# Layer 1's third adaLN projection made on VectorE instead of TensorE, and another order of blocks in layer 1's output projection

## The chip, the cores and the metric

The kernel runs on 1 core of one Trainium2 chip. The metric is device microseconds of one execution, the median of several runs; less is better.

## The reference, cut to what matters

Two layers of a transformer-like block over 256 latent tokens (`x`) and 256 context tokens (`ctx`), 1024 channels wide. Each layer begins with a small product, the adaLN projection: one conditioning vector for the latent stream and one for the context stream, each times a 1024 x 6144 matrix. Its six pieces scale and shift what goes into the token mixer (`sh1, sc1`), gate what comes out (`g1`), and do the same for the MLP (`sh2, sc2, g2`). The last layer drops the context stream after its token mixer has read it.

```python
for l in range(2):
    with_ctx = l < 1
    mod_lat = silu(c) @ w_ada[l] + b_ada[l]            # 1 x 6144; the same for c_ctx
    sh1, sc1, g1, sh2, sc2, g2 = split(mod_lat, 6)
    h = x * (1 + sc1) + sh1
    z = h @ w_in[l]                                     # q, k, v of A and B; xr, yr of the LRU; gates
    ya, yb = windowed_attention(z), global_attention(z) # GQA, 8 heads each
    yc = bidirectional_rg_lru(conv(xr)) * gelu(yr)
    o = (ga * (ya @ w_br_a) + gb * (yb @ w_br_b) + gc * (yc @ w_br_c)) @ w_out[l]
    x = layernorm(ALPHA * x + g1 * o)
    h = x * (1 + sc2) + sh2
    x = layernorm(ALPHA * x + g2 * (square(relu(h @ w_ff1[l])) @ w_ff2[l]))
```

## The kernel before, in words

**Weights in blocks.** Every weight matrix is cut into blocks of 1 MB (`plan_units`, a list in the order of use). A block is loaded into one of 3 `raw` buffers (`emit_dma`, L181, on SP's queue), then split into a high and a low part, `whi` and `wlo` (`queue_split`, L197: the cast on ScalarE, in layer 1's LRU half of it on VectorE; the subtraction on VectorE, L128), and TensorE takes three products per pair of tiles (high·high, high·low, low·high). `take` (L225) hands out a block and calls `prefetch` (L240), which calls `ada_step`, loads the block after next and queues the split of the next one. While `ada_q` (below) holds anything, `prefetch` loads up to two blocks ahead, otherwise three.

**The planner's clock.** `mm` (L89) adds an estimate to `self.pe` for every matmul: 0.42 per column of the moving operand, at least 107. Everything that is spread over time by hand hangs on this clock, not on the chip's: `tick` (L248) is called once per three matmuls, and starts pieces of splits and background steps. A block of 48 matmuls with 512 columns makes 48 x 215 = 10,322 units; with 256 columns (one stream only, as in layer 1 behind the LRU's inputs) 5,161.

**The adaLN projections.** Each layer's 6144 columns go in three projections of 2048 columns (blocks 0 to 3, 4 to 7 and 8 to 11 of 512 columns). A projection has 8 steps, one per 128 rows of the matrix. A step loads 1 MB into a `raw` buffer (the same three as the weights; `raw_ada`, L276), and then either

- on VectorE (`dve` = 1): 8 adds of 128x512, `ada_acc = raw_ada * silu + ada_acc` (L293; in the first step a plain product, L291), and after the eighth step `sums`: 8 matmuls with `pick` that sum over the partitions; or
- on TensorE (`dve` = 0): 4 matmuls per step straight from `raw_ada` (`mms`).

`ADA` says which projection is queued where. Before: layer 0's second and third at the start of layer 0's merge (`bra0`), layer 1's first and second at the start of layer 0's MLP (`mlp0`), both on VectorE; layer 1's third (blocks 8 to 11: `sc2` and `g2`) at the first gates of layer 1 (`ga1`), in its attention, on TensorE. `ada_step` (L335) runs one step at a `prefetch`, if the planner's clock has come to `ada_at`: it issues the adds still left of the step before, loads the next one, and sets `ada_at` to now plus the pace of the layer whose matrix it is. `tick` issues the adds one by one, the first 3000 units after the load, then one per gap:

```python
self.ada_at, self.ada_next, self.ada_gap = self.pe + pace, self.pe + 3000, (pace - 3000) / 8
```

**The order of the stages.** Layer 0: LRU, attention together with the merge, output projection, MLP (32 blocks of 512 columns: 16 of `f1`, 16 of `f2`). Layer 1: `lru` (L733) takes `xr0 xr1 yr0 yr1 kvA xr2 yr2 kvB xr3 yr3 qA0 qA1` in this order, and between them runs the LRU's chain on ScalarE, VectorE and GpSimd (`finish`, L758); then the attention, paired with `qB0 qB1` and the merge; the output projection (`wout`); the MLP. `xr` and `kv` are for both streams (512 columns), the others of layer 1 for the latent one.

**Layer 1's output projection and its tail.** `unit` (L1192) multiplies one half `h` of the 1024 rows of `w_out` for one block of 128 tokens `tb`; the two halves add up in one PSUM bank, and after the second `residual` (L1181) multiplies by the gate, adds, and takes the statistics, on VectorE. `tail_units` (L1290) does so for the last 512 columns (`keys[0]` and `keys[1]` are the halves), then `ln_z` (L1220) normalises, `ln_t` transposes on TensorE, and `ln_h` makes the MLP's input. The order before was tokens 2 half 0, tokens 2 half 1, tokens 3 half 0, tokens 3 half 1.

Of the kernel before, what the change touches and what calls it, by code (L numbers as in the profile page):

```python
# [47 lines left out]
class Kern:  # L48
# [220 lines left out]
    def ada_queue(self, l, blocks, dve):  # L269
# [18 lines left out]
        def add(k, j, s):  # L288
            acc, w, c = st["acc"][s][j], st[k][:, j, :], self.silu[:, k, s:s + 1]
            if k == 0:  # L290
                self.nc.vector.tensor_scalar(acc, w, c, None, op0=ALU.mult)  # L291
            else:
                self.nc.vector.scalar_tensor_tensor(acc, w, c, acc, op0=ALU.mult, op1=ALU.add)  # L293
# [24 lines left out]
        for k in range(KD):  # L318
            if dve:
                self.ada_q.append((lambda k=k: dma(k),  # L320
                                   [lambda k=k, j=j, s=s: add(k, j, s) for j in range(4) for s in range(2)],
                                   sums if k == KD - 1 else None, self.ADA_PACE[l]))
            else:
                self.ada_q.append((lambda k=k: dma(k), [], lambda k=k: mms(k), 0.0))

    ADA_PACE = (9500, 18000)

    ADA = (('bra0',0,4,1),('bra0',0,8,1),('mlp0',1,0,1),('mlp0',1,4,1),('ga1',1,8,0))

    def ada_start(self, at):  # L330
        for a, l, b, dve in self.ADA:
            if a == at:
                self.ada_queue(l, range(b, b + 4), dve)
# [956 lines left out]
    def tail_units(self, l, which, keys, xs):  # L1290


        final = l and which == 2
        if final:
            self.lnr = self.ln_rows(l, which)
        else:
            self.hn = [(self.g("h_hi", F32R), self.g("h_lo", F32R)) for _ in range(KD)]
        if l:
            ws = []
            for tb, j in ((2, 0), (2, 1), (3, 0), (3, 1)):  # L1300
                if tb == 2:
                    ws.append(self.take(keys[j]))
                self.unit(keys[j], ws[j], xs, (tb,), True)
                if j and not final:
                    self.ln_z(tb)
                elif j:
                    self.output(tb)
            if not final:
                self.ln_t(2)
                self.ln_t(3)  # L1310
                self.ln_h(l, which, 1)
                self.ln_late = lambda: None
        else:
            ws = [self.take(keys[0]), self.take(keys[1], prefetch=False)]
            for tb in range(2):
                for key, w in zip(keys, ws):
                    self.unit(key, w, xs, (tb,), True)
                if tb:
                    self.ln_t(0)
                self.ln_z(tb)  # L1320
            self.unit(keys[0], ws[0], xs, (2,), True)
            self.ln_t(1)
            self.ln_h(l, which, 0)
            self.unit(keys[0], ws[0], xs, (3,), True)
            self.prefetch()
            for tb in (2, 3):
                self.unit(keys[1], ws[1], xs, (tb,), True)
                self.ln_z(tb)

            def late():  # L1330
                self.ln_t(2)
                self.ln_t(3)
                self.ln_h(l, which, 1)

            self.ln_late = late
        if not final:
            self.h = self.hn
# [262 lines left out]
```

## Time and profile before

| | us |
|---|---|
| median of 3 runs | 1507.12 (1506.59 to 1509.21) |
| the profiled execution | 1507.38 |
| its span | 1505.6 |
| PE busy | 1455.2 (97%) |
| DVE busy | 1154.4 (77%) |
| ACT busy | 772.2 (51%) |
| POOL busy | 292.7 (19%) |

The span is the time from the first to the last instruction of one execution that the profiler recorded. PE is TensorE, DVE VectorE, ACT ScalarE, POOL GpSimd, SPq the queue that issues the loads. A row of the chain of work gives the time at which a piece starts and how long it takes; a row of groups gives the busy time, the mean ns of one instruction, and the idle time of its engine just before it with what ended that; PEclk is the granted TensorE clock, where 1.00 is 2.4 GHz.

### The profile page before, as it was taken

To read this page: it belongs to the slowest core of one execution; us is meant where nothing else is said; L and a number is where in the kernel's file an instruction comes from. 1 tells how busy PE (TensorE), PEld (TensorE's weight loads), DVE (VectorE), ACT (ScalarE), POOL (GpSimd) and SP (SyncE) were. 2 spreads that over 40 slices of the span, in tenths; PEclk is the share of its full clock that TensorE was granted. 3 is DMA by queue.
4 is the path that set the end of the run, shared out by engine and by line. 5 is a ranking of instruction groups with operands and counts; after the bars stand their busy time and mean duration, and the time that the engine had idled before them with its cause. 6 is when DMAs were issued, how large, how long until landed. Compare 5 with 4: busy or idle time off the path is not lost.

```text
span 1505.6 us, 22308 instructions
## 1 busy us (share of the span) xinstructions
PE 1455.2 (97%) x8364; PEld 1226.5 (81%) x8364; DVE 1154.4 (77%) x2179; ACT 772.2 (51%) x1594; POOL 292.7 (19%) x298
## 2 busy tenths in 40 slices
PE   7899999999999999899999999999899999899997
PEld 4688988777878879678878887897787899799986
DVE  4699987758688966977657768888989577886666
ACT  2698667565223327313323234587777655655452
POOL 0533422100000002711110301264411003031110
PEclk9999999999999999999999999999999999999999
DMA  9523310105557552444435343342345735755563
GB/s 325 194 85 111 113 57 29 43 29 172 169 190 247 198 198 95 159 160 159 162 112 192 116 168 110 107 143 74 123 144 178 243 109 185 251 169 186 181 193 112
DMA packets 156748, 225.69 MB, mean 150 GB/s; under 512 B 5840, under 2 KB 118992, under 8 KB 151520
## 3 DMA queue, kind: packets, MB, share of 16 engines
q1 hardware_dynamic: 156640, 224.27, 45.2%
q8 instruction: 65, 1.06, 0.3%
q14 instruction: 43, 0.35, 0.1%
HBM read 218.97 MB, written 5.28 MB: 149 GB/s over the span
## 4 chain that ended last, share of the span: by engine, by line
PE 80%; DVE 12%; ACT 4%; issue 2%; DMA 1%; POOL 0%; SPq 0%; DVEq 0%; ACTq 0%
PE ps_cm L92 42%; PE ps_tm L92 26%; DVE wlo L128 3%; PE ps_s L92 2%; PE ps_pv L92 2%; PE ps_pT L99 2%; PE ps_ada L92 2%; PE ps_gate L92 2%; DVE ada_acc L293 1%; DVE xc L647 1%; DMA raw_ada<-in_w_ada_dram 1%; PE ps_qT L99 1%; ACT L103 1%; DVE lru_q L718 1%; DVE lru_i L708 0%
## 5 line engine op out<-in xcount | busy, mean ns | idle before, releaser
L120 ACT CAST whi<-raw 128x512 fp32r<-128x512 f32 x521 | 300.1, 622 | 374.0 <-PE ps_tm L92 195.3
L128 DVE TENSOR_TENSOR wlo<-raw,whi 128x512 fp32r<-128x512 f32 x560 | 407.0, 753 | 103.2 <-ACT whi L120 98.0
L92 PE MATMUL ps_cm<-h_hi,wlo 128*128 128x256 f32 (+1 forms) x1216 | 406.9, 337 | 7.0 <-DVE wlo L128 6.9
L92 PE MATMUL ps_cm<-h_hi,whi 128*128 128x256 f32 (+1 forms) x1216 | 408.5, 340 | 3.0 <-ACT whi L120 2.0
L92 PE MATMUL ps_cm<-h_lo,whi 128*128 128x256 f32 (+1 forms) x1216 | 406.1, 336 | 0.2 <-POOL h_lo L1249 0.2
L92 PEld LDWEIGHTS ps_cm<-h_hi,whi 128*128 128x128 f32 x1216 | 230.4, 191 | 39.9 <-ACT whi L120 7.1
L92 PEld LDWEIGHTS ps_cm<-h_hi,wlo 128*128 128x128 f32 x1216 | 231.9, 191 | 34.3 <-DVE wlo L128 9.2
L92 PEld LDWEIGHTS ps_cm<-h_lo,whi 128*128 128x128 f32 x1216 | 232.0, 191 | 24.1 <-POOL h_lo L1249 0.7
L293 DVE SCALAR_TENSOR_TENSOR ada_acc<-raw_ada,silu,ada_acc 128x512 f32<-128x512 f32 x224 | 168.7, 799 | 49.6 <-DMA raw_ada<-in_w_ada_dram 49.4
L92 PE MATMUL ps_tm<-wlo,f_hi 128*128 128x512 f32 x384 | 150.2, 392 | 2.1 <-DVE wlo L128 2.1
L92 PE MATMUL ps_tm<-whi,f_hi 128*128 128x512 f32 x384 | 149.7, 390 | 0.0
L92 PE MATMUL ps_tm<-whi,f_lo 128*128 128x512 f32 x384 | 149.3, 389 | 0.0
L1188 POOL TENSOR_TENSOR x<-x,res 128x512 f32<-128x512 f32 x36 | 51.9, 1445 | 306.8 <-DVE res L1187 306.8
L92 PE MATMUL ps_tm<-wlo,h_hi 128*128 128x256 f32 x320 | 92.0, 287 | 6.1 <-DVE wlo L128 6.0
L92 PE MATMUL ps_tm<-whi,h_hi 128*128 128x256 f32 x320 | 92.9, 290 | 1.2 <-ACT lru_r L103 0.6
L92 PE MATMUL ps_tm<-whi,h_lo 128*128 128x256 f32 x320 | 91.4, 286 | 0.0
L92 PEld LDWEIGHTS ps_tm<-wlo,f_hi 128*128 128x128 f32 x384 | 72.1, 188 | 19.6 <-DVE wlo L128 5.2
L92 PEld LDWEIGHTS ps_tm<-whi,f_hi 128*128 128x128 f32 x384 | 72.1, 188 | 15.7 <-ACT whi L120 0.8
L103 ACT ACTIVATE p<-ps_s,mx 128x512 f32<-128x512 f32 (+1 forms) x96 | 58.5, 618 | 51.2 <-DVE mx L1001 29.9
L92 PEld LDWEIGHTS ps_tm<-whi,f_lo 128*128 128x128 f32 x384 | 72.1, 188 | 14.8
L685 POOL TENSOR_TENSOR lru_i<-lru_i,xc 128x512 f32<-128x512 f32 x32 | 52.8, 1680 | 89.3 <-ACT lru_i L103 89.3
L92 PEld LDWEIGHTS ps_tm<-wlo,h_hi 128*128 128x128 f32 x320 | 62.0, 194 | 7.7 <-DVE wlo L128 7.3
(173 smaller groups left out, 2449.5 us busy)
## 6 DMA issues: line engine op xcount, KB each, us to landing
raw<-in_w_ff_dram SPq DMA_DIRECT2D x64, 1024.0 KB, 5.5
raw<-in_w_in_dram SPq DMA_DIRECT2D x50, 1024.0 KB, 5.1
raw_ada<-in_w_ada_dram SPq DMA_DIRECT2D x40, 1024.0 KB, 5.0
w_ada<-in_w_ada_dram SPq DMA_DIRECT2D x32, 256.0 KB, 5.6
raw<-in_w_br_c_dram SPq DMA_DIRECT2D x8, 1024.0 KB, 5.7
raw<-in_w_out_dram SPq DMA_DIRECT2D x8, 1024.0 KB, 5.0
gw_raw<-in_v_gate_dram SPq DMA_DIRECT2D x16, 256.0 KB, 5.3
raw<-in_w_br_a_dram SPq DMA_DIRECT2D x8, 512.0 KB, 3.5
```

What stands on the lines that cost most here:

```text
L92: self.nc.tensor.matmul(out, lhsT, rhs, start=start, stop=stop, **kw)
L99: self.nc.tensor.transpose(out, in_, self.ident if n == 128 else self.ident[0:n, 0:n])
L103: ins = self.nc.scalar.activation(out, in_, func, **kw).ins
L120: self.nc.scalar.copy(out, in_)
L128: return self.nc.vector.tensor_tensor(lo, src, hi.bitcast(F32), op=ALU.subtract)
L293: self.nc.vector.scalar_tensor_tensor(acc, w, c, acc, op0=ALU.mult, op1=ALU.add)
L647: nc.vector.scalar_tensor_tensor(o, r3[:, :, lo_ + d:lo_ + d + n], w(j), o, op0=ALU.mult, op1=ALU.add)
L685: nc.gpsimd.tensor_tensor(ig, ig, self.xc[k[0]][0], op=ALU.mult)
L718: nc.vector.tensor_tensor_scan(h[:, cs][:, ::-1], r[:, cs][:, ::-1], ig[:, cs][:, ::-1], init, op0=ALU.mult, op1=ALU.add)
L1188: (nc.vector if last else nc.gpsimd).tensor_tensor(x, x, t, op=ALU.add)
```

## The change

Layer 1's third projection is queued at the start of layer 0's MLP behind the two that were there, and made on VectorE. The pace of layer 1's projections goes from 18,000 to 12,000 units of the planner's clock. In the tail of layer 1's output projection the two blocks of tokens alternate; the tail of the MLP keeps its order.

```diff
-    ADA_PACE = (9500, 18000)
+    ADA_PACE = (9500, 12000)

-    ADA = (('bra0',0,4,1),('bra0',0,8,1),('mlp0',1,0,1),('mlp0',1,4,1),('ga1',1,8,0))
+    ADA = (('bra0',0,4,1),('bra0',0,8,1),('mlp0',1,0,1),('mlp0',1,4,1),('mlp0',1,8,1))

         if l:
             ws = []
-            for tb, j in ((2, 0), (2, 1), (3, 0), (3, 1)):
+            for tb, j in ((2, 0), (2, 1), (3, 0), (3, 1)) if final else ((2, 0), (3, 0), (2, 1), (3, 1)):
                 if tb == 2:
                     ws.append(self.take(keys[j]))
                 self.unit(keys[j], ws[j], xs, (tb,), True)
```

## Rows read from the trace of the kernel before

**Rows 1.** The page: the chain that ended last, share of the span by engine
```profile
PE 80%; DVE 12%; ACT 4%; issue 2%; DMA 1%; POOL 0%; SPq 0%; DVEq 0%; ACTq 0%
```

**Rows 2.** Busy time of each engine by stretch of the span
```profile
core 0: us, PE busy (x) PEld busy (x) DVE busy (x) ACT busy (x) POOL busy (x), PEclk, DMA share, GB/s
575.00:653.00 78.00, 73.60 (x413) 62.14 (x412) 67.34 (x103) 35.69 (x76) 30.78 (x22) 1.00 0.45 149
653.00:929.00 276.00, 276.00 (x1230) 226.74 (x1229) 191.82 (x314) 77.59 (x142) 34.55 (x24) 1.00 0.45 151
933.00:979.00 46.00, 43.63 (x318) 38.93 (x317) 37.38 (x81) 27.68 (x58) 13.32 (x15) 1.00 0.31 104
979.00:1023.00 44.00, 44.00 (x293) 40.44 (x291) 38.95 (x57) 32.72 (x61) 28.59 (x24) 1.00 0.38 126
1023.00:1067.00 44.00, 37.49 (x217) 31.76 (x216) 38.41 (x63) 30.48 (x56) 20.94 (x26) 0.96 0.29 91
1067.00:1101.60 34.60, 29.43 (x196) 26.75 (x197) 31.56 (x50) 29.12 (x52) 9.29 (x8) 0.95 0.40 130
1101.60:1260.00 158.40, 156.21 (x1212) 136.00 (x1211) 125.29 (x299) 107.78 (x246) 19.12 (x20) 0.99 0.55 180
```

**Rows 3.** What PE waited for between 933 and 1101.6 us: us, times, longest
```profile
PE ps_tm L92 <- DVE wlo L128: 6.0, 5, 2.8
...
PE ps_cm L92 <- DVE wlo L128: 1.6, 1, 1.6
```

**Rows 4.** The chain of work in layer 1's attention: one of its eight adaLN steps
```profile
1192.79 1.00 PE ps_ada L92 x8
```

**Rows 5.** PE busy with the sums of one projection on VectorE, in layer 0's MLP
```profile
755.00:765.00 10.00, 1.92 (x16) 0.42 (x16) 0.68 (x1) 1.00 0.34 103
```

**Rows 6.** SP's queue: the first, second, third and last adaLN loads of 16 in layer 0's MLP
```profile
575.61 0.35 SPq L276 DMA_DIRECT2D raw_ada<-in_w_ada_dram  x1
...
599.68 0.33 SPq L276 DMA_DIRECT2D raw_ada<-in_w_ada_dram  x1
...
619.53 0.34 SPq L276 DMA_DIRECT2D raw_ada<-in_w_ada_dram  x1
...
897.35 0.34 SPq L276 DMA_DIRECT2D raw_ada<-in_w_ada_dram  x1
```

**Rows 7.** Groups on DVE between 653 and 930 us, in layer 0's MLP
```profile
L128 DVE TENSOR_TENSOR wlo<-raw,whi 128x512 fp32r<-128x512 f32 x100 | 70.0, 737 | 26.6 <-ACT whi L120 26.5
L293 DVE SCALAR_TENSOR_TENSOR ada_acc<-raw_ada,silu,ada_acc 128x512 f32<-128x512 f32 x93 | 68.6, 788 | 31.7 <-DMA raw_ada<-in_w_ada_dram 31.7
...
L291 DVE TENSOR_SCALAR ada_acc<-raw_ada,silu 128x512 f32<-128x512 f32 x8 | 4.8, 605 | 0.0
```

**Rows 8.** The costliest groups on DVE between 933 and 1101.6 us
```profile
L128 DVE TENSOR_TENSOR wlo<-raw,whi 128x512 fp32r<-128x512 f32 x60 | 46.1, 786 | 3.3 <-ACT whi L120 3.2
L122 DVE CAST whi<-raw 128x512 fp32r<-128x512 f32 x25 | 14.4, 604 | 5.7 <-PE ps_tm L92 4.9 <-PE ps_cm L92 0.7
L700 DVE SCALAR_TENSOR_TENSOR lru_q<-lru_q,lru_th 128x512 f32<-128x512 f32 x12 | 7.9, 686 | 5.1 <-ACT lru_q L694 5.0
```

**Rows 9.** DVE in order of time: five adds from 604.74 us, four from 815.00 us
```profile
604.74 6.52 DVE L293 SCALAR_TENSOR_TENSOR ada_acc<-raw_ada,silu,ada_acc 128x512 f32<-128x512 f32 x5
...
815.00 2.74 DVE L293 SCALAR_TENSOR_TENSOR ada_acc<-raw_ada,silu,ada_acc 128x512 f32<-128x512 f32 x4 [1.28 <-DMA raw_ada<-in_w_ada_dram]
```

**Rows 10.** POOL in order of time, 604 to 641 us
```profile
605.70 26.54 POOL L1268 TENSOR_TENSOR x<-x,ln_row 128x512 f32<-128x512 f32 x16 [13.97 <-DMA ln_row<-in_ln_g_dram]
```

**Rows 11.** The chain of work through the tail of layer 1's output projection
```profile
1284.59 16.36 PE ps_tm L92 x72
...
1300.98 0.70 DVE res L1187
...
1304.66 1.20 DVE wlo L128 x2
...
1306.51 1.20 DVE wlo L128 x2
1307.72 0.61 DVE res L1187
...
1311.11 0.45 PE ps_z L99 x2
```

**Rows 12.** What PE waited for between 1301 and 1335 us
```profile
PE ps_z L99 <- DVE x L1226: 3.9, 1, 3.9
```

## The prediction

> **What bounds the kernel now.** I read the chain of work first: 80% of it lies on PE and 12% on DVE [rows 1], so a change is worth what it takes from PE or makes PE wait. Then the stretches [rows 2]. In layer 0's MLP from 653 us PE is never idle (276.0 of 276 us) and DVE has 84 us to spare. In layer 1's LRU, 933 to 1101.6 us, it is otherwise: PE is busy 154.6 of 168.6 us and DVE 146.3, and in the second half PE falls to 37.5 of 44 and 29.4 of 34.6 us while DVE stands at 38.4 and 31.6. There PE waits above all for the low parts of the weights, which DVE makes [rows 3]. In layer 1's attention PE is full again (156.2 of 158.4), DVE busy 125.3.
>
> **Where the moved steps land.** The words of the change say layer 0's MLP; the planner's arithmetic says otherwise. A block there makes 10,322 units. The pace was 18,000: a step at every second block. The trace agrees: loads at 599.68 and 619.53 us, 16 of them from 575.61 to 897.35 us [rows 6]. The new pace of 12,000 is still more than 10,322, so a step still comes at every second block. One step is won at the start: the MLP's first two blocks are taken together and the next `prefetch` comes 17,195 units later (four passes of 2 x 24 matmuls with 256 columns, and 16 transposes), over 12,000 but under 18,000. So the 16 steps of the first two projections end one block sooner, and of the third projection's 8 steps only the first is loaded in the MLP, at the `prefetch` between its last units. I walked on through layer 1 with the same sum. Its `prefetch` calls let steps through after 22.8, 15.5, 20.6, 15.5, 15.5, 15.5 and 15.5 thousand units: at `xr1`, `yr1`, `xr2`, `kvB`, `xr3`, `qA0`, `qB0`. Seven of eight steps thus run in layer 1's LRU, and the last one's adds fall into the beginning of the attention.
>
> **The sum.**
>
> *Taken from layer 1's attention.* Eight steps on PE at about 1.0 us each on the chain [rows 4] (seven more are like it): -7.9 us. Added there: the sums, 1.9 us [rows 5]. PE is full in that stretch, so the net is -6.0 us. The bias add, the transposes, the gate's multiplication on POOL and its stores are the same in both. Bounds: 0, if PE then waits for something else in that stretch, and -8.
>
> *Added to DVE in the LRU.* 56 adds up to 1101.6 us: 8 products and 48 adds. In the MLP one add took 68.6/93 = 0.74 us and one product 4.8/8 = 0.60 [rows 7]. The split took 0.70 us there (70.0/100) and 0.77 in the LRU (46.1/60) [rows 7, 8], 1.1 times as much; so I take 0.81 and 0.66: 48 x 0.81 + 8 x 0.66 = 44 us. DVE is idle 168.6 - 146.3 = 22.3 us in that stretch [rows 2]. If every gap could be filled, DVE would need 146.3 + 44 = 190 us: +22. If it stayed at the 87% of now, 190/0.87 = 219: +50. Much of the idle time is waiting for ScalarE and PE in a chain (5.0 us for `lru_q`, 4.9 for PE, 3.2 for `whi` [rows 8]), so not all can be filled; but the queue is deeper with the adds in it, and at the 95% that lies between, it is 190/0.95 = 200: +32 us. I take that. PE cannot work ahead: its next block needs the low parts that stand behind the adds in DVE's queue, as do the convolution and the layer normalisation that feed it. The last step's 8 adds meet 33 us of idle DVE in the attention: 0.
>
> *Loads.* Eight loads of 1 MB and four of the bias move in SP's queue from between the attention's weights to between the LRU's. Each takes one of three `raw` buffers while its adds last, and `prefetch` loads two blocks ahead in the LRU instead of three. In the MLP DVE waited 31.7 us for such loads before 93 + 8 = 101 adds, or 2.5 us a step of 8 [rows 7], because the last adds of a step were issued just as the next load wanted their buffer. At the new gap of 1125 units they are out well before the next step, and DVE runs late in the LRU anyway: 0 taken, and 7 x 2.5 = 18 us as the upper bound.
>
> *Layer 0's MLP.* Cadence the same, adds closer together, DVE has room: 0 from 653 us. Before that POOL's two passes over `x` run for 26.5 us [rows 10] and PE lost 4.4 us [rows 2]. The adds that met them move by a block: between -4 and +4, taken as 0.
>
> *The tail of layer 1's output projection.* Twelve matmuls take 16.36/72 x 12 = 2.7 us [rows 11]. Tokens 2 are finished one unit later, at 1303.7 instead of 1300.98 us; PE ends as before. Before, DVE went through tokens 2 and four splits (2.4 us) from 1300.98 on, came to tokens 3 at 1307.72, and PE's transposes went on at 1311.11, after 3.9 us of waiting [rows 11, 12]. After, DVE has from 1303.7: twice the 2.1 us of `residual`, twice 0.4 of moments, 1.3 for the first normalisation, 0.4 for the next, some 7 us with its waits for ScalarE, which ends at 1311 again. The splits go into the gap before, or else stand in the way. Bounds: -1.4 to +2.4; taken as 0.
>
> Sum: +32 - 6 = +26 us on the profiled execution's 1507.4, 0.3 us above the median: **1533 us**. Its own range: with the ends of DVE's share, +22 - 8 to +50 - 6, and 4 us for the MLP and the tail, 1517 to 1555.
>
> **The rivals.**
>
> *DVE takes it (the other side).* The gaps fill, and what is over slides behind the splits into the attention, where DVE has 33 us. Then only PE's gain is left: 1507.4 - 6 = 1501 us. For it: from 979 to 1023 us DVE is 89% busy and PE not idle at all [rows 2], so a full DVE need not stop PE. Against it: the adds come from the same program as the splits and stand between them, not behind, and the excess over all gaps is 22 us. It decides from the point where DVE's overrun stays under the attention's gain of 6 us, that is, where the adds cost less than 28 us together, 0.5 each; the fastest row gives 0.68 (2.74/4 [rows 9]).
>
> *Half of each.* The overrun is as large as the gain: 1507 within 3 us.
>
> *The port.* Where POOL worked at the same time, five adds took 6.52 us, 1.3 each, against 0.68 when it was quiet [rows 9, 10]. POOL is busy 72 of 168.6 us in the LRU [rows 2]. If adds waited like that for the 43% of time that POOL works: 0.43 x 1.3 + 0.57 x 0.68 = 0.95 each, 48 x 0.95 + 8 x 0.8 = 52 us; with DVE at 90%, (146.3 + 52)/0.90 = 220, +51: 1507 + 51 - 6 = 1552 us. The splits have two inputs in the same memory too, and grew by a tenth only, which is why I don't take it. The Trainium skill (SBUF — State Buffer, Who interferes with whom) has a rule that would go further: a VectorE instruction with two inputs in SBUF and a GpSimd instruction that reads SBUF share one read port, and the second to start waits for the whole of the other. By that rule every add that meets a POOL instruction would be held; the rows with five adds in 6.52 us agree, the splits' mean in the LRU agrees only in part.
>
> *The buffers.* The raw buffer held by the adds, the shorter look-ahead and eight more accumulators in a pool of 63 make loads late as well: 12 blocks in the LRU, each waiting some 2.5 us as the adds did, +30 on the forecast: 1563 us.
>
> **The numbers.** Chances: the forecast 0.65, DVE takes it 0.12, half of each 0.06, the port 0.12, the buffers 0.05. The forecast's range goes to 1555 and the port's 1552 lies in it; for the buffers I go to 1560; below, I go to 1504 to take in the middle case and leave out the fast one. Measurement can tell 0.2%, 3 us, from no change. Slower: 0.65 + 0.12 + 0.05 = 0.82. Same 0.06, faster 0.12.
>
> **What would show it.** Right: 17 loads of `raw_ada` in layer 0's MLP and 7 in layer 1 up to the attention; L293 on DVE between 933 and 1130 us; DVE at 93% or more there and PE waiting for `wlo` by some 30 us more; 64 fewer matmuls from `raw_ada` and PE full in the attention, which is 6 us shorter. In the tail PE's wait for `x` stays near 3.9 us. Wrong: if more than 17 loads stand in layer 0's MLP, my walk through the planner is wrong; if the LRU has the adds but is under 10 us longer, the price on PE is.

## The result and the profile after

The changed kernel takes 1530.27 us (1529.55 to 1531.34), the kernel before 1506.86 on the same chip: a ratio of 1.0153, 95% interval 1.0135 to 1.0170. The change costs 23.4 us. The forecast was 1533. The profiled execution of the changed kernel took 1530.17 us, its span is 1528.3.

Where the moved steps went is read from SP's queue of the changed kernel (the first three adaLN loads of layer 0's MLP; then the first and the last of the seven in layer 1).

```profile
575.41 0.35 SPq L276 DMA_DIRECT2D raw_ada<-in_w_ada_dram  x1
584.29 0.33 SPq L276 DMA_DIRECT2D raw_ada<-in_w_ada_dram  x1
605.55 0.33 SPq L276 DMA_DIRECT2D raw_ada<-in_w_ada_dram  x1
...
950.28 0.33 SPq L276 DMA_DIRECT2D raw_ada<-in_w_ada_dram  x1
...
1100.37 0.34 SPq L276 DMA_DIRECT2D raw_ada<-in_w_ada_dram  x1
```

Seventeen loads stand in layer 0's MLP, four up to 650 us and thirteen after it, and seven in layer 1's LRU. The second load comes 9 us after the first instead of 24 [rows 6]; from there on the steps keep their distance of two blocks.

To see where the time went, three marks are compared: layer 1's first attention scores, the first matmul of its output projection, and the end. This is the tile `ps_s` in the kernel before and in the changed one (duration min/median/max in ns, then the first and the last start).

```profile
L92 PE MATMUL ps_s<-kT,qT x64: 387/396/628, 1100.4 to 1240.6; 128*128 128x512 f32 x64
```

```profile
L92 PE MATMUL ps_s<-kT,qT x64: 387/395/497, 1126.5 to 1265.6; 128*128 128x512 f32 x64
```

The scores start 26.1 us later. The output projection starts at 1284.4 and 1307.0 us, 22.6 later, and the end is 22.7 later. So the way to layer 1's first scores lost 26 us, nearly all of it in the LRU, the attention gave 3.5 back, and the rest did nothing. Here is the same by stretches, first of the kernel before (LRU up to the scores, then attention up to the output projection; columns as in [rows 2]), then of the changed kernel, with layer 0's MLP ahead.

```profile
930.00:1100.40 170.40, 156.36 (x1029) 139.36 (x1028) 145.12 (x245) 121.89 (x230) 74.15 (x75) 0.98 0.33 109
...
1100.40:1284.40 184.00, 181.81 (x1421) 161.43 (x1421) 141.63 (x334) 121.45 (x275) 21.58 (x21) 0.99 0.54 178
```

```profile
575.00:650.00 75.00, 70.63 (x404) 61.10 (x403) 68.14 (x105) 33.67 (x73) 30.21 (x21) 1.00 0.48 155
650.00:927.00 277.00, 276.95 (x1234) 227.73 (x1234) 193.15 (x309) 78.84 (x145) 39.36 (x24) 1.00 0.46 150
...
930.00:1126.50 196.50, 164.44 (x1023) 147.48 (x1021) 188.77 (x307) 121.44 (x227) 80.55 (x75) 0.92 0.40 134
...
1126.50:1307.00 180.50, 175.04 (x1376) 158.80 (x1374) 143.58 (x336) 120.70 (x275) 20.18 (x21) 1.00 0.43 138
```

In the LRU DVE's busy time rises by 43.7 us, from 145.1 to 188.8, and its share from 85% to 96%. ScalarE does the same work in both. The two groups on DVE that matter there, in the changed kernel:

```profile
L128 DVE TENSOR_TENSOR wlo<-raw,whi 128x512 fp32r<-128x512 f32 x60 | 47.4, 806 | 0.4 <-ACT whi L120 0.3
L293 DVE SCALAR_TENSOR_TENSOR ada_acc<-raw_ada,silu,ada_acc 128x512 f32<-128x512 f32 x53 | 42.3, 828 | 0.5 <-DMA raw_ada<-in_w_ada_dram 0.5
```

53 adds take 42.3 us, 0.80 each (busy time by count; the 828 ns of a single record are more, since neighbours overlap), and DVE waits for almost nothing before them. What it waited for before the splits, 3.3 us [rows 8], is down to 0.4. And PE, between 930 us and the scores, in the changed kernel:

```profile
PE ps_tm L92 <- DVE wlo L128: 10.9, 7, 6.7
PE ps_cm L92 <- DVE wlo L128: 9.1, 4, 3.5
PE ps_tm L92 <- ACT whi L120: 3.4, 1, 3.4
```

It waited 7.6 us for the low parts of the weights [rows 3]; now it is 20.0. The longest of these waits shows how: five adds stand on DVE right before the split that PE needs (PE's row, then DVE's).

```profile
1118.16 0.58 PE L92 MATMUL ps_tm<-wlo,h_hi 128*128 128x256 f32 x1 [6.65 <-DVE wlo L128]
...
1114.11 3.39 DVE L293 SCALAR_TENSOR_TENSOR ada_acc<-raw_ada,silu,ada_acc 128x512 f32<-128x512 f32 x5
1117.43 0.68 DVE L128 TENSOR_TENSOR wlo<-raw,whi 128x512 fp32r<-128x512 f32 x1
```

Of the 26.1 us PE is idle for 18.0 more (32.1 instead of 14.0) and busy for 8.1 more, with nearly the same number of matmuls (1029 before, 1023 now). The granted TensorE clock in that stretch is 0.92 of full speed against 0.98: behind some pauses PE works for a few microseconds at the lower of its two levels, 1.2 instead of 2.4 GHz. Here is one such pause of the changed kernel, and the work behind it.

```profile
1030.50:1034.50 4.00, 0.39 (x1) 0.19 (x1) 3.59 (x10) 1.86 (x4) 0.00 (x0) 1.00 0.40 111
1035.00:1041.00 6.00, 5.78 (x27) 5.78 (x28) 6.00 (x13) 3.51 (x7) 4.92 (x4) 0.50 0.51 178
```

### The profile page after: what moved, and what is told of

It is laid out like the page before. It is cut to its first block, busy times and chain, and to the rows that moved or that the text cites. A ratio compares the mean times of both kernels' runs of the same rounds, so it can differ in the third digit from the quotient of the medians.

```text
span 1528.3 us, 22254 instructions
## 1 busy us (share of the span) xinstructions
PE 1456.5 (95%) x8316; PEld 1232.6 (81%) x8316; DVE 1203.2 (79%) x2243; ACT 772.0 (51%) x1594; POOL 302.3 (20%) x298
## 5 line engine op out<-in xcount | busy, mean ns | idle before, releaser
L293 DVE SCALAR_TENSOR_TENSOR ada_acc<-raw_ada,silu,ada_acc 128x512 f32<-128x512 f32 x280 | 213.6, 805 | 65.1 <-DMA raw_ada<-in_w_ada_dram 65.0
L1188 POOL TENSOR_TENSOR x<-x,res 128x512 f32<-128x512 f32 x36 | 56.7, 1584 | 298.9 <-DVE res L1187 298.9
L92 PEld LDWEIGHTS ps_tm<-whi,h_hi 128*128 128x128 f32 x320 | 63.8, 199 | 5.2 <-ACT whi L120 3.6
```

The costliest lines, as they stand in the source:

```text
L92: self.nc.tensor.matmul(out, lhsT, rhs, start=start, stop=stop, **kw)
L1188: (nc.vector if last else nc.gpsimd).tensor_tensor(x, x, t, op=ALU.add)
```

## The experiments

All times are compared with runs of the kernel before on the same chip. "Late" means layer 1's first scores against 1100.4 us in the profile of the kernel before.

**1. All steps really in the MLP.** The next due time is counted from the last due time instead of from the load, so that the remainder of a block isn't lost.

```diff
-    ADA_PACE = (9500, 12000)
+    ADA_PACE = (9500, 13000)
-            self.ada_at, self.ada_next, self.ada_gap = self.pe + pace, self.pe + 3000, (pace - 3000) / 8
+            due = self.ada_at if self.pe - self.ada_at < pace else self.pe
+            self.ada_at, self.ada_next, self.ada_gap = due + pace, self.pe + 3000, (pace - 3000) / 8
```

> The changed kernel, but the next step's due time is counted from the last due time and not from the moment of the load, at a pace of 13,000: 24 steps in 24 x 13,000 = 312,000 units, so all 24 loads stand in layer 0's MLP (some 331,000 units long) and none in layer 1's LRU. Theory (the adds in the LRU cost the time, nothing else does): the LRU is as long as in the kernel before, DVE in the MLP goes from 70% to about 85% and PE stays full there, the attention gains its 6 us, so 1507 - 6 - 1 = 1500 us, 0.995 to 0.997 of before. Rival (loads, accumulators and the pace cost time wherever they are): 1510 to 1525. Rival (the MLP has no room for 64 more adds): PE idle in the MLP by 10 us or more, 1510 or more.

Measured: 1504.28 against 1508.28 us, 0.9972 (0.9963 to 0.9981). It beats both kernels, but the first by 4.0 us instead of the 7 that were expected; 0.9972 is at the far edge of the range of 0.995 to 0.997. Its stretches: the MLP from 650 us, then the LRU, then the attention. (The MLP ends 6 us later, so the LRU is counted from 936.)

```profile
650.00:750.00 100.00, 99.67 (x448) 80.80 (x447) 86.90 (x148) 28.60 (x52) 14.07 (x9) 1.00 0.58 193
750.00:850.00 100.00, 100.00 (x451) 81.36 (x450) 80.44 (x122) 28.60 (x52) 19.30 (x12) 1.00 0.50 164
850.00:930.00 80.00, 80.00 (x362) 64.81 (x361) 66.99 (x105) 22.29 (x41) 8.68 (x5) 1.00 0.51 171
...
936.00:1106.00 170.00, 153.54 (x1014) 139.12 (x1013) 144.68 (x258) 122.32 (x230) 71.67 (x74) 0.98 0.33 109
...
1106.00:1280.90 174.90, 170.75 (x1354) 157.98 (x1353) 139.12 (x319) 120.45 (x275) 19.55 (x20) 1.00 0.42 137
```

DVE is 84% busy in the MLP, and PE is idle for 0.3 of these 280 us. The LRU is as long as before, 170.0 us. The attention is 9.1 us shorter, since nothing of the projection is left in it. The scores are 5.6 us late; the output projection starts 3.5 us early. The third projection's sums (1.9 us a projection [rows 5]) and transposes now stand ahead of the scores, and the granted clock from 575 to 650 us is 0.98 instead of 1.00 [rows 2]; whether that is all of the 5.6 was not traced. PE waits for DVE 4.9 us between 575 and 940 us, against 4.3 before. So the 64 products and adds cost PE under 1 us of waiting here; in the changed kernel's LRU they cost 26 us.

**2. The loads in the same places, the work on TensorE.**

```diff
-    ADA = (..., ('mlp0',1,8,1))
+    ADA = (..., ('mlp0',1,8,0))
-                self.ada_q.append((lambda k=k: dma(k), [], lambda k=k: mms(k), 0.0))
+                self.ada_q.append((lambda k=k: dma(k), [], lambda k=k: mms(k), self.ADA_PACE[l]))
```

> The changed kernel with the third projection's 24 loads at the very same places (7 of 8 in the LRU), but each step's 4 matmuls on TensorE instead of 8 adds on VectorE. Theory (VectorE's 44 us): the LRU shrinks to within 5 us of before, because PE has some 14 us of idle time there for its 8 us; the attention keeps its gain of 6 to 8 us; about 1500 to 1504 us. Rival (the loads in the LRU: a raw buffer less, a shorter look-ahead): still 1520 to 1530 us.

Measured: 1511.31 us, 1.0020 (1.0011 to 1.0030). The scores are 8.4 us late, not 26.1, so most of the loss is DVE's work and not the loads. But the theory's number is missed: the LRU should have hidden the 8 us of matmuls in PE's idle time and did not.

```profile
930.00:1108.80 178.80, 168.08 (x1090) 139.22 (x1088) 147.19 (x248) 121.88 (x230) 72.35 (x76) 0.99 0.45 148
```

PE is busy 11.7 us more than before in that stretch and the stretch is 8.4 us longer. The projection's 64 matmul records alone keep PE busy for 14.3 us there, not 8; in the attention of the kernel before it was 9.6. PE's idle time in the LRU (14.0 us before) is not free either.

**3. Narrow adds.**

```diff
+                if l == 1 and blocks[0] == 8:
+                    acc, w = acc[:, 0:64], w[:, 0:64]
                 self.nc.vector.scalar_tensor_tensor(acc, w, c, acc, op0=ALU.mult, op1=ALU.add)
```

> The changed kernel with the third projection's 56 adds made over 64 of 512 columns (the products of the first step stay whole): this leaves out seven eighths of that sum for the other columns. Loads, instruction counts and places as in the changed kernel; DVE's extra work in the LRU falls from 47 us to some 48 x 0.2 + 8 x 0.5 = 14 us, less than the 22 us of idle time there. Theory (DVE's busy time): the LRU is 2 to 8 us longer than before, 1503 to 1510 us. Rival (instructions and waits count, not their length): 1520 or more.

Measured: 1513.69 us, 1.0039 (1.0025 to 1.0052), scores 10.1 us late: between the two.

```profile
930.00:1110.50 180.50, 158.71 (x1027) 142.96 (x1027) 161.85 (x310) 122.38 (x229) 76.92 (x75) 0.94 0.45 152
```

DVE is busy 16.7 us more than before (a narrow add takes 17.5/56 = 0.31 us, more than the 0.2 assumed). That is less than its 25.3 us of idle time, and yet the stretch is 10.1 us longer. The number and places of the instructions are those of the changed kernel; their length makes the difference between 10 and 26.

**4. The loads alone.** As experiment 3, with one narrow add per step.

```diff
+                if l == 1 and blocks[0] == 8:
+                    if j or s:
+                        return
+                    acc, w = acc[:, 0:64], w[:, 0:64]
```

> The changed kernel, but of the third projection's 56 adds only one per step is left, over 64 of 512 columns; the 8 products of the first step and all loads stay. This leaves out nearly all of that projection's sum. DVE's extra work from the first load in the LRU on is under 2 us. Theory (DVE's busy time alone): layer 1 up to the attention's first scores is within 3 us of before, about 1503 to 1505 us. Rival (the loads themselves cost some 7 us: of the 8.4 and 10.1 us by which the scores start late with matmuls or narrow adds in the adds' place, most would be left): 1509 to 1512 us, scores 6 to 9 us late.

Measured: 1505.53 us, 0.9987 (0.9978 to 0.9997), scores 1.8 us late.

```profile
930.00:1102.20 172.20, 157.21 (x1020) 141.74 (x1019) 151.29 (x260) 120.49 (x226) 71.47 (x74) 0.95 0.48 158
```

With all loads, accumulators and the shorter look-ahead in place the LRU is 1.8 us longer, with 6.2 us more of DVE. The rival of late loads falls, but for one thing: with one add a step a raw buffer comes free sooner than in the changed kernel. The next experiment is about that.

**5. A fourth raw buffer and the longer look-ahead.**

```diff
-        self.pg = ec(tc.tile_pool(name="gen", bufs=63))
+        self.pg = ec(tc.tile_pool(name="gen", bufs=59))
-        self.pr = ec(tc.tile_pool(name="raw", bufs=3))
+        self.pr = ec(tc.tile_pool(name="raw", bufs=4))
-        self.emit_dma(i + 3 if not self.ada_q else i + 2)
+        self.emit_dma(i + 3)
```

> The changed kernel with four raw buffers instead of three (taken from the general pool, 59 instead of 63) and the look-ahead of three blocks kept while adaLN steps are queued. Theory (DVE is full in the LRU, 97%, so earlier weights don't help): 1527 to 1531 us. Rival (the raw buffer that the adds hold and the shorter look-ahead are part of the loss, some 7 of 23 us): 1520 to 1525 us.

Measured: 1532.39 us, 1.0159 (1.0142 to 1.0176), scores 27.6 us late, DVE busy 189.6 of 198.0 us. In the changed kernel one weight load did come late, and ScalarE waited for it:

```profile
1119.18 1.66 ACT L120 CAST whi<-raw 128x512 fp32r<-128x512 f32 x3 [8.47 <-DMA raw<-in_w_in_dram]
```

With four buffers this wait is gone, and PE still waits 19.4 us for the low parts of the weights (20.0 in the changed kernel). Earlier weights are worth nothing where DVE is full. (The general pool is smaller here, which may cost something of its own; it would have to hide a gain of the same size.)

**6. Three steps in the LRU instead of seven.** The kernel of experiment 1 at a pace of 16,500.

> The kernel whose steps are counted from the last due time, at a pace of 16,500: 21 of 24 loads fall into layer 0's MLP and three into the LRU (xr1, yr1, xr2), with 24 adds of 0.8 us there, 19 us, less than the 22 us that DVE is idle in it. Theory (the adds fill the gaps first, only the excess costs): the scores start 3 to 7 us later than before, the time is 1502 to 1506 us. Rival (each add costs its own length or half of it wherever it stands in the LRU: 3/7 of 26 us is 11): scores 10 us or more late, 1509 to 1513 us.

Measured: 1513.99 us, 1.0043 (1.0028 to 1.0058), scores 19.2 us late in the profile.

```profile
930.00:1119.60 189.60, 167.36 (x1057) 151.02 (x1056) 176.17 (x302) 123.54 (x231) 74.17 (x75) 0.92 0.38 126
...
PE ps_adaT L99 <- DVE ada_rows L305: 7.4, 1, 7.4
```

Not all of the 19.2 us belongs to the LRU. As in experiment 1 the MLP ends later; its first transposes start at 930.57 us instead of 925.45. Counted from there (the kernel before, then this one) the scores are 14.1 us late, with 26.7 us more of DVE:

```profile
925.45:1100.40 174.95, 160.91 (x1054) 142.91 (x1053) 148.94 (x254) 122.65 (x231) 74.15 (x75) 0.98 0.32 106
...
930.57:1119.60 189.03, 166.79 (x1054) 150.62 (x1053) 175.60 (x300) 123.54 (x231) 74.17 (x75) 0.92 0.37 125
```

The profiled execution took 1517.52 us, 3.5 more than the median, so 14.1 may be up to 3.5 too high. Either way the theory's 3 to 7 us fall.

Two things stand in the stretch. It holds 32 adds, those of the step before too, and DVE has 31.1 us more than before from 930 us on. And the projection now ends inside the LRU: its transposes stand in PE's queue and wait 7.4 us for a row that DVE makes late, a wait that the changed kernel doesn't have there.

**7. A step at every block of the MLP.** The changed kernel with `ADA_PACE = (9500, 10000)`, just under the 10,322 units of a block.

> The changed kernel with a pace of 10,000 instead of 12,000, under the 10,322 units of a block: one step at every block of layer 0's MLP, so the 24 steps end after 24 blocks of 32 and none reaches layer 1. Theory (what counts is that no add stands in the LRU, and the MLP's DVE has just enough room): DVE about 97% busy in the first three quarters of the MLP, PE idle there by 0 to 8 us; 1500 to 1508 us. Rival (DVE is already too full there, splits come late at each block): 1512 or more.

Measured: 1519.45 us, 1.0084 (1.0062 to 1.0105). No add stands in the LRU, but layer 1's first gates start 20.9 us late (996.4 against 975.5). The theory's 1500 to 1508 us is missed and the rival's time came, though late splits are only part of the reason. The MLP from 650 to 750 us, and what PE waited for longest:

```profile
650.00:750.00 100.00, 93.16 (x403) 72.43 (x402) 88.73 (x149) 26.40 (x48) 13.16 (x8) 0.98 0.55 181
...
PE ps_ada L92 <- DVE ada_acc L293: 7.2, 2, 4.3
```

The sums reach PE's queue right behind the last adds, which DVE hasn't made yet, and PE stands. Against experiment 1 only the spacing differs: 24 steps in 24 blocks or in 32. So the MLP has room for all 24 steps, but only if they are spread over it. This wait and the splits' (6.6 us) explain 14 of the 20.9. Experiment 1, which has the same sums ahead of that mark, is 5.5 us late there (981.0), and that is most of the rest.

**8 to 10. The other parts alone.** The old order in the tail of the changed kernel; the pace alone and the alternating order alone in the kernel before.

> The changed kernel with the old order of blocks in the tail of layer 1's output projection. Theory: the order is worth nothing within 1 us, 1529 to 1531 us; PE's wait for the normalised x before the transposes is 3.9 us again (in the changed kernel the same stretch is 0.2 us longer than before). Rival (the new order hides a loss or a gain of 2 us): 1528 or 1532.

> The kernel before with a pace of 12,000 alone: the third projection stays on TensorE in the attention, the first two end one block of the MLP sooner. Theory: -1 us (the MLP of the changed kernel is 1.1 us shorter), 1505 to 1507 us. Rival (denser adds cost PE time): 1509 or more.

> The kernel before with the alternating order alone. Theory: no difference, 1506 to 1508 us. Rival (it is worth 2 us either way and another loss covers it in the changed kernel): 1505 or 1509.

Measured: 1530.06 us (1.0144, 1.0130 to 1.0158) with the old order, as good as the changed kernel's 1530.27; 1507.97 (1.0001, 0.9992 to 1.0010) with the pace alone; 1509.33 (1.0012, 1.0002 to 1.0021) with the new order alone. The pace alone did not give the 1 us that was expected. The new order alone lies above the 1506 to 1508 us that were expected and at its rival's 1509; the interval leaves out 1 by 0.02%, while in the changed kernel the order makes no difference that can be told. So neither part is worth more than about 0.2%. In the profiles the way from the first matmul of the output projection to the MLP's first is 28.3 us before, 28.4 in the changed kernel and 28.4 with the new order alone. The changed kernel's transposes in the tail:

```profile
1331.55 3.81 PE L99 MATMUL ps_z<-ident,x 128*128 128x128 f32 x16 [2.62 <-DVE x L1226]
```

PE waits 2.6 us instead of 3.9 [rows 12], but all 16 transposes come behind the wait; before, half of them came ahead of it.

## Why the prediction was right

**Where the steps land: right to the block.** The walk through the planner's units gave 17 loads in the MLP and 7 in the LRU; so it came. The 17,195 units of the start are those of three passes and 16 transposes (3 x 48 x 107.5 + 16 x 107), as in the program, and not of the four that the prediction names; four would make 22,355, over the old pace of 18,000 too.

**The adds in the LRU: the price right, the sum a fifth too large.** An add was put at 0.81 us and took 0.80. DVE's extra work was put at 44 us and is 43.7, which is partly luck: 53 adds and 8 products stood in the stretch instead of 56 together, 47.1 us by themselves, and DVE's other work took 3.4 us less of its time. DVE's share was chosen between 87% and 100%, as 95%, and is 96%. The term was +32 and measures +26.1. The difference has three parts of about 2 us each: DVE's busy time (188.8 us instead of 190.3), its share, and the stretch before (170.4 us to the scores instead of 168.6).

**The gaps: the form of the term was wrong, though its size held.** The sum took idle time as something that fills first, so that the lower bound was 22 us and smaller doses would be free. The runs show otherwise. DVE's extra time in the LRU and the delay of the scores:

| | DVE extra, us | scores late, us | per us |
|---|---|---|---|
| loads alone (experiment 4) | 6.2 | 1.8 | 0.3 |
| narrow adds (3) | 16.7 | 10.1 | 0.60 |
| three steps (6), from the MLP's end | 26.7 | 14.1 | 0.53 |
| the changed kernel | 43.7 | 26.1 | 0.60 |

Beyond the smallest dose each microsecond of DVE costs 0.5 to 0.6, from far below the 25 us that were idle. The best pair is the narrow adds against the changed kernel, with the same instructions in the same places: 27.0 us of DVE cost 16.0, 0.59 each. DVE's gaps are waits in a chain with ScalarE and PE: work put in front of a gap is hidden, work behind it is not, and where the adds fall is not chosen by the gaps. That the gaps take some four tenths of what comes is shown, and one wait behind five adds too; that the chain makes all of it so is argued. One sign of the prediction was not met: PE was to wait for `wlo` by some 30 us more, and it was 12.4 (20.0 against 7.6). The rest of the 26.1 us is 5.6 us of other idle time of PE and 8.1 us more of busy time at the lower mean clock, for which the sum had no term.

**The attention: the term was -6 and measures -3.5.** PE has 6.8 us less to do there (181.8 to 175.0), about as forecast; but its idle time goes from 2.2 to 5.5 us, 2.5 of it waits for what ScalarE makes of the scores (`p`), which were not there before. The bound of -8 in that term was passed by experiments 1, 6 and 7 (-9.1 each), where nothing of the projection is left in the attention. The total came out nearer (+23.4 for +26) than its terms, since a loss 6 us too large and a gain 2.5 us too large partly cancel.

**The loads: taken as 0, right within 2 us.** Experiments 4 (1.8 us) and 5. The step was wrong in one thing: DVE's waits for `raw_ada` in the MLP should have gone with the earlier adds. They grew, from 31.7 us [rows 7] to 48.9 in the changed kernel:

```profile
L293 DVE SCALAR_TENSOR_TENSOR ada_acc<-raw_ada,silu,ada_acc 128x512 f32<-128x512 f32 x88 | 68.0, 827 | 48.9 <-DMA raw_ada<-in_w_ada_dram 48.9
```

It cost nothing, since PE is never idle there (276.95 of 277 us).

**The MLP and the tail: taken as 0**, and -1.1 us (the transposes at the MLP's end start at 927.96 instead of 929.07 us) and +0.1.

**The rivals.** "DVE takes it" falls: it needed adds that cost less than 28 us together, and they cost 43.7; so does "half of each", which stood at 1507 us. "The buffers" fall with experiments 4 and 5. "The port" was too dear, 0.95 us an add. The adds of the changed kernel between 931.9 and 1119.6 us (min/median/max in ns):

```profile
L293 DVE SCALAR_TENSOR_TENSOR ada_acc<-raw_ada,silu,ada_acc x53: 732/739/1782, 955.3 to 1116.8; 128x512 f32<-128x512 f32 x53
```

Seven took over 1 us, three of them more than twice the median. In each of the seven a GpSimd instruction ran at the same time, as here (DVE, then POOL):

```profile
992.50 1.78 DVE L293 SCALAR_TENSOR_TENSOR ada_acc<-raw_ada,silu,ada_acc 128x512 f32<-128x512 f32 x1
...
992.12 1.62 POOL L631 TENSOR_TENSOR gw<-gw_raw,gw 128x512 fp32r<-128x512 f32 x1
```

The Trainium skill (SBUF — State Buffer, Who interferes with whom) says that a VectorE instruction with two SBUF inputs contends with a GpSimd instruction that reads SBUF, that the port is locked, and that the order of issue decides which of the two waits. The seven adds agree with that. But it would be wrong to charge the price of a contended add to the whole share of time that GpSimd is busy (41% of the stretch): that gave 0.95 us an add, and 0.80 was measured.

## What to carry to other kernels

A pace that is checked only where a block of work begins is rounded up to whole blocks: 12,000 against blocks of 10,322 was the same as 18,000 but for one step at the start, and the steps that the name of the change put into one stage ran in the next. Count the next due time from the last one, spread the steps over the whole stage, and look at what the engine does in the stage where they land. In this kernel an engine at 85% was as good as full where others wait for it in a chain: more than half of what was added there came out as time, long before its idle time ran out. The same work, spread over a stage where that engine was at 70%, was nearly free; packed into three quarters of that stage it was not (experiment 7).

## What the runs showed of the hardware that was not expected

PE's idle time in the LRU was as little use as DVE's: matmuls that kept PE busy for 14.3 us, in a stretch where it had been idle for 14.0, made it 8.4 us longer (experiment 2). A VectorE add over 64 columns is not an eighth of one over 512 but more than a third: 0.31 against 0.80 us here, and by their medians in the traces 274 against 739 ns; the narrow ones' row:

```profile
L295 DVE SCALAR_TENSOR_TENSOR ada_acc<-raw_ada,silu,ada_acc x56: 269/274/1339, 956.3 to 1101.3; 128x64 f32<-128x64 f32 x56
```
